# A finite-difference gradient: hand-placed semaphores and one difference pass over both rows of a tile

## The chip, the cores and the metric

The kernel runs on one core of one Trainium2 chip. The metric is the device time of a whole execution in microseconds. "Before" is the median of six runs; one execution was also recorded by the hardware profiler, and that record is the source of every duration below. The engines that matter here are VectorE (DVE), ScalarE (ACT), GpSimd (POOL) and SyncE (SP, which computes nothing and here issues loads), and the 16 DMA engines that move data between HBM and the on-chip memory SBUF.

## The reference

```python
def setup_inputs():
    return {
        "x": np.random.randn(8192, 8192).astype(np.float32),
    }

def reference(x: np.ndarray) -> np.ndarray:
    return np.gradient(x, axis=1)
```

Along each row of 8192 numbers the result is (x[j+1] - x[j-1]) / 2 inside, x[1] - x[0] at the left end and x[8191] - x[8190] at the right end. The rows don't depend on each other. 268 MB are read and 268 MB are written, with two small operations for each element.

## The kernel before

The 8192 rows are cut into 32 sets (`nsets`) of 256 rows. In a set each of the 128 partitions holds two neighbouring rows (`R = 2`), one behind the other, so a set is a tile of 128 x 16384 fp32 numbers (`W = 16384`), 64 KB in each partition and 8 MB in all. A buffer `b` of the pool has 64 more columns (`SH`): the input lies at columns 64 to 64 + W, and the result is written from column 0 on. So the result overwrites the buffer's own input, 64 columns behind the place that is being read, and one buffer serves for input and output. The pool has three such buffers (`bufs=3`); they are called slots below.

For each set, in program order:

- SP issues the load of the whole tile (line 66). The last set's load is cut into two, one for each row.
- The function `diff` works on half a row at a time (`step = m // 2`), four times for a tile, and on a quarter of a row, eight times, for the last tile. It subtracts on DVE over the inside of the piece (line 46); where the piece begins or ends a row, a one-column subtraction on DVE makes the end column (lines 39 and 52). Then ACT multiplies the inside of the piece by 0.5 in place (line 57).
- ACT issues the store of the whole tile (line 78) after its last multiplication. For the last tile it issues a store of each quarter row (line 74).

So one piece's multiplication on ACT runs while DVE subtracts the next. Loads go through SP's DMA queue and stores through ACT's. The instructions of an engine run in the order in which the program lists them (`manual_schedule`), while the waits between engines and DMAs are put in by the framework from the tiles that are read and written. A load into a slot waits until the store of the tile that the slot held three sets earlier has landed.

Of the kernel before, what the change touches and what calls it, by code (L numbers as in the profile page):

```python
# [1 line left out]

# [4 lines left out]


@with_exitstack
def kernel(  # L10
    ctx: ExitStack,
    tc: tile.TileContext,
    x: bass.AP,
    out: bass.AP,
):

    nc = tc.nc
    P = nc.NUM_PARTITIONS
    n, m = x.shape
    R = 2
    SH = 64
    W = R * m
    nsets = n // (P * R)

    x_sets = x.rearrange("(s p t) m -> s p (t m)", p=P, t=R)
    out_sets = out.rearrange("(s p t) m -> s p (t m)", p=P, t=R)  # L30

    pool = ctx.enter_context(tc.tile_pool(name="pool", bufs=3))

    def diff(b, c0, c1):

        lo, hi = c0, c1
        if c0 % m == 0:
            lo = c0 + 1
            nc.vector.tensor_sub(  # L39
                out=b[:, c0:lo],  # L40
                in0=b[:, SH + c0 + 1 : SH + c0 + 2],
                in1=b[:, SH + c0 : SH + c0 + 1],
            )
        if c1 % m == 0:
            hi = c1 - 1
        nc.vector.tensor_sub(  # L46
            out=b[:, lo:hi],
            in0=b[:, SH + lo + 1 : SH + hi + 1],
            in1=b[:, SH + lo - 1 : SH + hi - 1],
        )  # L50
        if hi < c1:
            nc.vector.tensor_sub(  # L52
                out=b[:, hi:c1],
                in0=b[:, SH + hi : SH + c1],
                in1=b[:, SH + hi - 1 : SH + c1 - 1],
            )
        nc.scalar.mul(out=b[:, lo:hi], in_=b[:, lo:hi], mul=0.5)  # L57

    with tc.manual_schedule():
        for i in range(nsets):  # L60
            last = i == nsets - 1
            b = pool.tile([P, SH + W], x.dtype)

            ls = m if last else W
            for c0 in range(0, W, ls):
                nc.sync.dma_start(  # L66
                    out=b[:, SH + c0 : SH + c0 + ls],
                    in_=x_sets[i, :, c0 : c0 + ls],
                )
            step = m // 4 if last else m // 2  # L70
            for c0 in range(0, W, step):
                diff(b, c0, c0 + step)
                if last:
                    nc.scalar.dma_start(
                        out=out_sets[i, :, c0 : c0 + step], in_=b[:, c0 : c0 + step]
                    )
            if not last:
                nc.scalar.dma_start(out=out_sets[i], in_=b[:, 0:W])


# [1 line left out]
_INS = ['x']  # L82
_OUTS = [((8192, 8192), 'float32')]


# [23 lines left out]
```

## Time and profile before

| what | value |
|---|---|
| median of six runs | 1251.67 us (1246.27 to 1253.14) |
| the profiled execution's own time | 1246.27 us |
| its span, from first to last instruction | 1244.5 us |
| bytes read and written | 268.44 MB and 268.44 MB, 431 GB/s over the span |
| DVE subtraction of 128 x 4095 (line 46) | 124 times, 4424 ns each |
| DVE one-column passes (lines 39 and 52) | 128 times, 155 and 159 ns |
| ACT multiplication of 128 x 4095 (line 57) | 124 times, 3616 ns each |
| load of 8 MB, from issue to landing | 45.2 us, median of 31 |
| store of 8 MB, from issue to landing | 48.5 us, median of 31 |
| DVE idle before line 39, waiting for a load | 640.0 us in 33 waits |
| SP waiting for a store to land before it issues a load | 1126.7 us in 29 waits |

The profiled execution is the fastest of the six. Time from issue to landing is not the time that a transfer takes alone: two transfers in two queues share the DMA engines, and one behind another in the same queue waits for it. An engine's idle time costs nothing as long as another part of the machine sets the end.

### The profile page before, as it was taken

The page shows a single profiled execution, that of the slowest core. Times are in us where ns is not written, and L with a number is a line of the kernel's source. Part 1 is how long each engine was busy: PE and PEld are TensorE (multiplying, and loading weights), DVE is VectorE, ACT ScalarE, POOL GpSimd, SP SyncE. Part 2 cuts the span into 40 slices and gives each one's busy share as a digit, 9 for nine tenths or more (in the row PEclk, how much of TensorE's full clock was granted, in tenths as well). Part 3 has the DMA queues.
Part 4 walks back from the last instruction along what each step waited for, and adds up shares of the span by engine and source line. Part 5 has one row for each costly group of instructions (what it writes and reads, how often), then busy time and mean ns, then how long its engine had stood idle before and what let it go on. Part 6 is the DMA issues. An engine that isn't in the chain of part 4 may idle for free.

```text
span 1244.5 us, 665 instructions
## 1 busy us (share of the span) xinstructions
DVE 584.5 (47%) x260; ACT 464.9 (37%) x133; POOL 0.2 (0%) x4
## 2 busy tenths in 40 slices
DVE  2950554335543355533555335553355533455353
ACT  1731442234422344323443234432344322443252
POOL 0000000000000000000000000000000000000000
DMA  9999999999999999999999999999999999999998
GB/s 404 434 438 426 421 438 434 438 438 436 426 426 436 434 438 436 438 438 436 419 432 438 434 438 436 438 436 428 428 432 434 438 436 436 438 438 423 427 433 379
DMA packets 10373, 536.92 MB, mean 431 GB/s; under 512 B 1152, under 2 KB 1152, under 8 KB 1152
## 3 DMA queue, kind: packets, MB, share of 16 engines
q1 hardware_dynamic: 4752, 268.44, 50.0%
q10 hardware_dynamic: 5616, 268.44, 49.8%
q14 instruction: 5, 0.04, 0.0%
HBM read 268.44 MB, written 268.44 MB: 431 GB/s over the span
## 4 chain that ended last, share of the span: by engine, by line
DMA 75%; DVE 16%; another core or an unknown queue 4%; ACT 3%; issue 0%; SPq 0%; DVEq 0%
DMA out_dram<-b 38%; DMA b<-in_x_dram 37%; DVE b L46 16%; ACT b L57 3%; DVE b L39 0%; DVE b L52 0%; SPq L66 0%; DVEq L39 0%
## 5 line engine op out<-in xcount | busy, mean ns | idle before, releaser
L57 ACT ACTIVATE b<-b 128x4095 f32<-128x4095 f32 (+1 forms) x132 | 463.6, 3512 | 745.3 <-DVE b L46 745.3
L46 DVE TENSOR_TENSOR b<-b 128x4095 f32<-128x4095 f32 (+1 forms) x132 | 567.0, 4295 | 4.5
L39 DVE TENSOR_TENSOR b<-b 128x1 f32<-128x1 f32 x64 | 9.9, 155 | 640.0 <-DMA b<-in_x_dram 640.0
L52 DVE TENSOR_TENSOR b<-b 128x1 f32<-128x1 f32 x64 | 10.2, 159 | 2.2
L57 ACT ACT_TABLE_LOAD x1 | 1.3, 1283 | 22.9 <-DMA b<-in_x_dram 22.9
L93 POOL MEMSET const-bfloat16-1.0<- 128x1 bf16 x1 | 0.1, 102 | 0.0
L93 POOL MEMSET const-uint8-127<- 128x1 uint8 x1 | 0.1, 102 | 0.0
L93 POOL MEMSET const-float32-0.0<- 128x1 f32 x1 | 0.1, 99 | 0.2 <-issue 0.2
L93 POOL MEMSET const-float32-1.0<- 128x1 f32 x1 | 0.1, 99 | 0.0
## 6 DMA issues: line engine op xcount, KB each, us to landing
b<-in_x_dram SPq DMA_DIRECT2D x2, 4096.0 KB, 44.9
out_dram<-b ACTq DMA_DIRECT2D x8, 1024.0 KB, 19.0
b<-in_x_dram SPq DMA_DIRECT2D x31, 45.2
out_dram<-b ACTq DMA_DIRECT2D x31, 48.5
```

Source lines behind the costliest of these rows:

```text
L39: nc.vector.tensor_sub(out=b[:, c0:lo], in0=b[:, SH + c0 + 1 : SH + c0 + 2], in1=b[:, SH + c0 : SH + c0 + 1],)
L46: nc.vector.tensor_sub(out=b[:, lo:hi], in0=b[:, SH + lo + 1 : SH + hi + 1], in1=b[:, SH + lo - 1 : SH + hi - 1],)
L52: nc.vector.tensor_sub(out=b[:, hi:c1], in0=b[:, SH + hi : SH + c1], in1=b[:, SH + hi - 1 : SH + c1 - 1],)
L57: nc.scalar.mul(out=b[:, lo:hi], in_=b[:, lo:hi], mul=0.5)
L93: nc = _bacc.Bacc("TRN2", target_bir_lowering=False, num_devices=1)
```

## The change

The three slots become three fixed tiles, and all waits are written out by hand with semaphores: `ld[k]` and `st[k]` count the landings of loads and stores of slot k, `aside`, `passed`, `halved` and `placed` count finished instructions of POOL, DVE, ACT and of the engine that places the end columns. A small tile `ends` holds the end columns of all sets, and a tile `top` takes a running maximum that nobody reads.

For each tile:

- POOL waits for the load, and computes the four end columns of a partition (two rows, left and right) in one subtraction with strided access into `ends` (`put_aside`).
- DVE waits for POOL, and makes one pass from column 1 to column 16383 of the tile, across the border between the two rows. Where two rows meet, the pass writes values that the placing replaces.
- In two tiles of three this pass is `tensor_tensor_reduce`: subtract, multiply by 0.5, write, and keep a maximum. In the third (`i % 3 == 1`) it is the plain subtraction, and ACT multiplies the whole tile in one instruction.
- POOL or ACT (`placer`) copies the four end columns from `ends` to their places.
- The store of the whole tile is issued by ACT, except for the last three sets, where SP issues it. The last set is loaded whole, worked on row by row with `tensor_tensor_reduce`, and stored row by row from SP.
- On SP, load i + 3 is issued after the program's lines for tile i, and waits for store i to land.

```diff
-    pool = ctx.enter_context(tc.tile_pool(name="pool", bufs=3))
+    pool = ctx.enter_context(tc.tile_pool(name="pool", bufs=1))
+    slots = [pool.tile([P, SH + W], f32, name=f"slot{k}", tag=f"slot{k}") for k in range(NB)]
+    ends = pool.tile([P, nsets, R, 2], f32, name="ends", tag="ends")
+    top = pool.tile([P, nsets + R], f32, name="top", tag="top")
...
+        def load(i):
+            k = i % NB
+            if st_n[k]:
+                nc.sync.wait_ge(st[k], 16 * st_n[k])
+            nc.sync.dma_start(out=slots[k][:, SH : SH + W], in_=x_sets[i]).then_inc(ld[k], 16)
+            ld_n[k] += 1
+
+        def put_aside(i):
+
+            k = i % NB
+            xin = slots[k][:, SH : SH + W].rearrange("p (t m) -> p t m", m=m)
+            nc.gpsimd.wait_ge(ld[k], 16 * ld_n[k])
+            return done(
+                nc.gpsimd.tensor_sub(
+                    out=ends[:, i, :, :],
+                    in0=xin[:, :, 1 : m : m - 2],
+                    in1=xin[:, :, 0 : m - 1 : m - 2],
+                ),
+                aside,
             )
...
+        def work(i, r0, nr, ready, by_act, placer, storer, sem):
+
+            b = slots[i % NB]
+            c0, c1 = r0 * m + 1, (r0 + nr) * m - 1
+            mid = b[:, c0:c1]
+            after = b[:, SH + c0 + 1 : SH + c1 + 1]
+            before = b[:, SH + c0 - 1 : SH + c1 - 1]
+            nc.vector.wait_ge(*ready)
+            if by_act:
+                at = done(nc.vector.tensor_sub(out=mid, in0=after, in1=before), passed)
+                nc.scalar.wait_ge(*at)
+                at = done(nc.scalar.mul(out=mid, in_=mid, mul=0.5), halved)
+            else:
+                j = i + r0
+                at = done(
+                    nc.vector.tensor_tensor_reduce(
+                        out=mid,
+                        in0=after,
+                        in1=before,
+                        scale=0.5,
+                        scalar=0.0,
+                        op0=op.subtract,
+                        op1=op.max,
+                        accum_out=top[:, j : j + 1],
+                    ),
+                    passed,
+                )
+            taken = passed[0], passed[1]
+            res = b[:, r0 * m : (r0 + nr) * m].rearrange("p (t m) -> p t m", m=m)
+            to, of = res[:, :, 0 : m : m - 1], ends[:, i, r0 : r0 + nr, :]
+            placer.wait_ge(*at)
+            copy = nc.gpsimd.tensor_copy if placer is nc.gpsimd else nc.scalar.copy
+            at = done(copy(out=to, in_=of), placed[placer])
+            storer.wait_ge(*at)
+            storer.dma_start(
+                out=out_sets[i, :, r0 * m : (r0 + nr) * m],
+                in_=b[:, r0 * m : (r0 + nr) * m],
+            ).then_inc(sem, 16)
+            return taken
 
-    with tc.manual_schedule():
+        for i in range(NB):
+            load(i)
         for i in range(nsets):
...
+            k = i % NB
+            ready = put_aside(i)
+            if i < nsets - 1:
+                by_act = i % 3 == 1
+                placer = nc.scalar if i % 3 == 2 or i % 6 == 0 else nc.gpsimd
+                storer = nc.scalar if i + NB < nsets else nc.sync
+                work(i, 0, R, ready, by_act, placer, storer, st[k])
+                st_n[k] += 1
+            else:
+                for r in range(R):
+                    ready = work(i, r, 1, ready, False, nc.gpsimd, nc.sync, st_rows[r])
+            if i + NB < nsets:
+                load(i + NB)
+        for r in range(R):
+            nc.sync.wait_ge(st_rows[r], 16)
+        for k in range(NB):
+            nc.sync.wait_ge(st[k], 16 * st_n[k])
```

## The prediction

> **What bounds the kernel now.** I read the page's head first, for who is busy, then the DMA slices and queues, then the stretch-by-stretch windows, then the chain and the timeline of single tiles.
>
> ```profile
> span 1244.5 us, 665 instructions
> DVE 584.5 (47%) x260; ACT 464.9 (37%) x133; POOL 0.2 (0%) x4
> ...
> GB/s 404 434 438 426 421 438 434 438 438 436 426 426 436 434 438 436 438 438 436 419 432 438 434 438 436 438 436 428 428 432 434 438 436 436 438 438 423 427 433 379
> ...
> q1 hardware_dynamic: 4752, 268.44, 50.0%
> q10 hardware_dynamic: 5616, 268.44, 49.8%
> q14 instruction: 5, 0.04, 0.0%
> ```
>
> The reader is to see that no engine is busy for half of the span, while the two data queues together hold the 16 DMA engines for 50.0 + 49.8 = 99.8% of it. Instruction fetches are 5 packets of 0.04 MB: shorter programs free nothing there.
>
> ```profile
> core 0: us, DVE busy (x) ACT busy (x) POOL busy (x), PEclk, DMA share, GB/s
> 22.80:42.10 19.30, 18.24 (x8) 13.12 (x5) 0.00 (x0) 1.00 1.00 435
> 1124.30:1162.90 38.60, 18.25 (x8) 14.46 (x4) 0.00 (x0) 1.00 1.00 433
> 1162.90:1201.50 38.60, 24.93 (x12) 18.28 (x6) 0.00 (x0) 1.00 1.01 434
> 1201.50:1240.20 38.70, 12.28 (x9) 11.46 (x6) 0.00 (x0) 1.00 0.98 418
> ```
>
> The first of these stretches has almost only loads, the second a load and a store side by side, and both run at 433 to 435 GB/s. So one queue with work in it fills the DMA engines as well as two do, and the last stretch, at 418, is the only one of the four that gives anything away.
>
> ```profile
> 1047.13 46.03 DMA b<-in_x_dram
> ...
> 1115.22 47.68 DMA out_dram<-b
> ```
>
> That is the chain (start, length, what), and the next is the timeline of one tile.
>
> ```profile
> 1131.88 0.16 DVE L39 TENSOR_TENSOR b<-b 128x1 f32<-128x1 f32 x1 [20.15 <-DMA b<-in_x_dram]
> ...
> 1153.82 0.34 ACTq L78 DMA_DIRECT2D out_dram<-b  x1
> ```
>
> In the chain a slot is loaded in 46.0 us, worked on for 22.0 (from 1093.2 to 1115.2) and stored in 47.7: 115.8 us, three times 38.6, because three slots take turns. The chain puts 15.7% of the span on DVE, but that is the slot's turn and not the limit. A tile's 8.39 MB passes alone in 19.3 us (the two first landings, 22.8 and 42.1), so of the 93.7 us of transfer in a turn 55 are spent sharing with the other slots. Work may lengthen by most of that before the queues run dry. The tile's data are there at 1131.9, its store is issued at 1153.8, and DVE had been idle for 20.15 us.
>
> The floor: 32 tiles x 38.6 us = 1236. The rest of the span, about 8.5 us, is some 3.5 at the head (0.7 to the first issue, and the first landing 22.1 later instead of 19.3) and some 5 at the tail and in slow slices. That is all that any change of the compute can win.
>
> [...] (4424 ns for 4095, 2292 for 2047, hence 1.041 ns an element and 0.16 us fixed). [...]
>
> **The change part by part.**
>
> *The passes.* Four DVE passes of 4424 ns and four one-column ones (157 ns) a tile become one pass of 16382 elements: 16382 x 1.041 + 0.16 = 17.2 us at full rate. Ten tiles keep ACT's multiplication, 16382 x 0.833 + 0.20 = 13.9 us (slope from 3616 and 1910 ns). In 21 tiles and the two rows of the last one the new DVE form halves as well. At full rate DVE has 32 x 17.2 = 551 us of work and ACT some 145: both fall, and neither bounds. [...] I take the full rate[...].
>
> *POOL and the placers.* A subtraction of four elements a partition, then a copy of four on POOL or ACT. The nearest rows are DVE's one-column pass (0.16) and POOL's memset (0.1); I take 0.5 us for each, with 0.2 and 3 as ends. The subtraction is new on the path from landing to store: DVE waits for POOL, and behind POOL's copy of one tile stands the subtraction of the next. On SP load i+3 still waits for store i; ACT's stores stand behind its copies and, for ten tiles, behind the 13.9 us.
>
> *The slot's turn.* Landing to store becomes 0.5 + 17.2 + 0.5 + hand-overs = about 18.7 us (22.0 before), and 18.7 + 13.9 = 33 in ACT tiles. Transfers alone need 2 x 19.3, so 115.8 - 33 - 38.6 leaves 44 us of sharing. Hidden; price nothing. Cover fails where a tile's work passes about 36 us (38.6 less the 2.8 that an empty queue needs to start, from 22.1 - 19.3): then all three slots can be without a transfer.
>
> *The head.* Tile 0 lands at 22.8, its store goes out near 41.5 (44.8 before), while load 2 is still running. Tile 1: 42.1 + 33 = 75; store 0, sharing with load 2, lasts to about 80. No gap.
>
> *The tail.* The last tile is loaded whole, and stores 29, 30 and the two rows move from ACT's queue to SP's, behind load 31. Take the old clock: at 1163.0 store 28 has landed and load 31 goes out. Load 30 is done by 1166, load 31 by 1185, stores 29 and 30 by 1224, the rows by 1234 and 1244. DVE works on tile 30 from 1166 to 1184 and on the rows to 1204, so row 0's data are ready 25 us before their turn; SP, waiting in order, holds nothing back. The stores of 1024 KB, whose 2 us windows average about 425 GB/s over 17 us, go: 0.4 us. The dip before them, 303 and 348 GB/s in 1220 to 1224, may go too: 0.5. Fewer small things in between: 0.3, by guess. Sum: -1.2 us, with 0 and -2.7 as ends (the latter is a span of 1236 + 3.5 + 2.3).
>
> *Instruction counts.* The engines' own instructions fall from 260 + 133 + 4 to 33 on DVE, 26 on ACT and 49 on POOL, with the waits beside them; the queue-14 line prices it at nothing.
>
> So the span of 1244.5 becomes 1243.3, and the profiled execution, 1246.27, 1245.1. The median of the runs, 1251.67, stands 5.4 us above that execution, which is the lowest of the six; I carry the difference over: **1250.5 us**.
>
> **The rivals.**
>
> *Half-rate pass (slower).* Passes of 34.3 us. Start: tile 0's store goes out at 22.8 + 0.5 + 34.3 + 0.5 = 58, load 2 ends at 61, store 0 at about 80; tile 1, behind tile 0 on DVE and then on ACT, is ready only at 89, so DMA is empty until load 3 starts: 2.8 us, and once more a turn later. Tail: tile 30's pass ends at 1201, row 0 at 1218, row 1 at 1235.5, after its turn at 1234; with placing and a restart about 4 us lost. Sum 2 x 2.8 + 4 - 1.2 = +8: **1259.5**. It decides from 25 us a pass at the start (54.9 + the pass against 80) and 33 at the tail.[...]
>
> *POOL late.* A subtraction or copy that takes 6 us or more[...] brings ACT tiles to 39 us, past the 36. Two or three restarts, 3 to 8 us: **1256**.[...]
>
> *More won than the span shows (faster).* The whole tail goes, -2.7, and of the 5.4 us that ordinary runs have over the profiled one some belong to the many small instructions: **1246.5**. Nothing in the trace shows such a share.
>
> **How the numbers follow.** Hidden, no change: 0.54. Half rate: 0.22. POOL late: 0.10. Faster: 0.14. About 0.3%, or 3.8 us, is what a measurement here tells from nothing; the first case lies within it (own range 1248 to 1253), the second and third are slower, the fourth faster: 0.14, 0.54, 0.32. The range of 1246 to 1260 holds the first and third, most of the fourth and half of the second.
>
> **What would show it.** Right: slices of 430 to 438 GB/s to the end, no dip in the first 130 us, a reducing pass near 17.2 us, DVE idle before landings, last stores back to back. Wrong: a pass near 34 us, POOL lines of several us in the chain, DMA slices below 400 near 80, 120 or 1234 us.

## The result

The changed kernel is slower: 1264.01 us median against 1251.99, ratio 1.0083 with an interval of 1.0067 to 1.0098. The forecast was 1250.5 us, no change that can be measured, and its range ended at 1260: it missed on both counts. The profiled execution of the changed kernel took 1263.34 us with a span of 1261.5, 17.0 us more than the span of before. Medians here and below are over all runs, while the ratios leave out runs more than 1.5% above the fastest of their kernel (6 of the changed kernel's 31, none of the 67 before), so the two need not agree to the last tenth of a per cent.

The first view is the head of the page and its DMA slices, of the changed kernel.

```profile
span 1261.5 us, 256 instructions
DVE 551.5 (44%) x56; ACT 143.0 (11%) x27; POOL 18.4 (1%) x53
...
GB/s 401 430 432 432 432 432 432 432 424 436 434 432 432 432 432 432 430 405 441 438 438 384 434 432 418 401 432 432 409 432 436 434 414 434 434 432 432 399 401 397
...
q1 hardware_dynamic: 5184, 293.60, 54.5%
q10 hardware_dynamic: 4176, 243.27, 45.0%
```

DVE and ACT do less than before, POOL's work is 1% of the span, and the program has 256 instructions instead of 665. The same bytes are moved, but at 426 GB/s over the span instead of 431: slices of 405, 384, 401, 409 and 414 stand among slices of 432, some three or four slices (of 31.5 us) apart, and the last three are near 400. So time is lost in the transfers, in places, and not to a compute engine that works too long.

It is not lost mainly by DMA engines that stand idle. The two queues' packets hold them for 54.5 + 45.0 = 99.5% of 1261.5 us, that is 1255 us; before it was 99.8% of 1244.5, or 1242 us. So about 13 of the 17 us are packets that take longer for the same bytes. The windows of the long middle part (us, busy of DVE, ACT and POOL, clock, DMA share, GB/s), before and after, say the same: the share is 1.00 in both, and less is moved.

```profile
150.00:1150.00 1000.00, 474.05 (x207) 372.43 (x103) 0.00 (x0) 1.00 1.00 434
150.00:1150.00 1000.00, 440.16 (x42) 127.06 (x21) 7.69 (x39) 1.00 1.00 428
```

The next view is the groups by line with shapes kept apart (busy us, mean ns of one, idle before).

```profile
L102 DVE CUSTOM_DVE_ANT_0 slot<-slot 128x16382 f32<-128x16382 f32 x21 | 361.7, 17224 | 461.1 <-POOL ends L79 461.1
L96 DVE TENSOR_TENSOR slot<-slot 128x16382 f32<-128x16382 f32 x10 | 172.2, 17224 | 201.4 <-POOL ends L79 201.4
L98 ACT ACTIVATE slot<-slot 128x16382 f32<-128x16382 f32 x10 | 138.5, 13854 | 576.8 <-DVE slot L96 576.8
...
L119 POOL COPY slot<-ends 128x2 f32<-128x2 f32 x2 | 8.9, 4447 | 8.8 <-DVE top L102 8.8
L79 POOL TENSOR_TENSOR ends<-slot 128x4 f32<-128x4 f32 x32 | 6.4, 200 | 793.7 <-DMA slot<-in_x_dram 793.7
...
L119 POOL COPY slot<-ends 128x4 f32<-128x4 f32 x15 | 2.9, 192 | 398.7 <-ACT slot L98 312.1 <-DVE top L102 86.7
```

The new one-pass form takes 17224 ns, to the nanosecond as long as the plain subtraction of the same size: the half-rate rival is out. POOL's small operations take 0.2 us: the rival of a late POOL is out for the whole tiles too. On whole tiles every operation of the sum had the forecast duration within 0.3 us, and the sum was still wrong.

Two of the places, in windows of one tile's DMA time, with the same columns:

```profile
738.00:776.60 38.60, 17.22 (x1) 6.27 (x1) 0.20 (x1) 1.00 1.00 431
776.60:815.20 38.60, 17.23 (x2) 7.78 (x2) 0.39 (x2) 1.00 0.95 389
815.20:853.90 38.70, 17.23 (x2) 0.00 (x0) 0.39 (x2) 1.00 1.00 434
853.90:892.50 38.60, 17.23 (x1) 4.05 (x1) 0.20 (x1) 1.00 1.00 433
892.50:931.10 38.60, 17.23 (x2) 10.00 (x2) 0.39 (x2) 1.00 0.98 406
```

In this stretch two of the five windows move less, and they are those in which ACT finishes a whole tile. At 389 GB/s about 10% is missing, while the DMA share is only 5% lower. The chain runs through that tile's slot, slot 1, in every turn:

```profile
708.99 43.78 DMA slot<-in_x_dram
...
753.07 17.23 DVE slot L96
...
770.33 13.86 ACT slot L98
...
784.47 42.17 DMA out_dram<-slot
826.65 44.24 DMA slot<-in_x_dram
...
902.59 42.53 DMA out_dram<-slot
```

This turn, from store to store, is 902.59 - 784.47 = 118.1 us; before, the median is 115.9. The work in it grew from 22.0 to 31.7 us, and load and store together shrank only from 93.7 to 86.4. Turns differ: the nine between the ten stores of slot 1 take 12.1 us more than before in all, and a single one up to 3.9.

How late that store is shows in the timeline, of ACT's and SP's DMA issues. SP's line is the load that waits for the previous tile's store, so it tells when that one landed. First the changed kernel, then the kernel before:

```profile
784.47 0.34 ACTq L121 DMA_DIRECT2D out_dram<-slot  x1
...
786.52 0.33 SPq L70 DMA_DIRECT2D slot<-in_x_dram  x1
```

```profile
766.65 0.34 ACTq L78 DMA_DIRECT2D out_dram<-b  x1
...
776.60 0.33 SPq L66 DMA_DIRECT2D b<-in_x_dram  x1
```

Before, the next store was put in the queue 10.0 us ahead of the landing of the one in front of it; now it is 2.1 us. I call this the lead of a store. Its median over eight turns of slot 1 is 10.0 us before and 1.9 after; the two tiles without ACT have 16.8. While the stores' queue has no next transfer, only one load moves, and it is about to end too (at 791.5 us in this turn): its successor waits for the same store.

Two microseconds are too few, as the single packets in the traces show (each belongs to the DMA engine whose previous packet ended when it began). A packet of 64 KB usually holds one DMA engine for 2418 ns. Half of the 16 engines have moved their last packet of a store 4.5 us (before) or 6.5 us (slot 1 now, both medians) ahead of the landing that SP waits for. So when slot 1's store is issued now, 15 or 16 engines have no store packet left, half of them for 2.1 to 8.1 us already; before, it was never more than two engines. The packets after such a restart take up to 4.3 us. Between the head and the tail (tiles 3 to 28), in the 18 us after each issue of slot 1, what packets take beyond 2418 ns adds up to 0.4 to 2.0 us for each DMA engine; for the other two tiles, and for all tiles before, to 0.2 at most. So an empty stores' queue goes with slow packets more than with idle engines.

### The profile page after: what moved, and what is told of

It reads as the page before. It is cut to its first block, busy times and chain, and to the rows that moved or that the text cites. A ratio compares the mean times of both kernels' runs of the same rounds, so it can differ in the third digit from the quotient of the medians.

```text
span 1261.5 us, 256 instructions
## 1 busy us (share of the span) xinstructions
DVE 551.5 (44%) x56; ACT 143.0 (11%) x27; POOL 18.4 (1%) x53
## 3 DMA queue, kind: packets, MB, share of 16 engines
q1 hardware_dynamic: 5184, 293.60, 54.5%
## 4 chain that ended last, share of the span: by engine, by line
DMA 70%; DVE 14%; ACT 11%; POOL 1%; issue 0%; SPq 0%
DMA slot<-in_x_dram 36%; DMA out_dram<-slot 34%; DVE slot L96 14%; ACT slot L98 11%; POOL slot L119 1%; DVE slot L102 1%; POOL ends L79 0%; SPq L70 0%; SPq L172 0%; DVE top L102 0%; SPq L46 0%
## 5 line engine op out<-in xcount | busy, mean ns | idle before, releaser
L102 DVE CUSTOM_DVE_ANT_0 slot<-slot 128x16382 f32<-128x16382 f32 (+1 forms) x23 | 379.1, 16482 | 466.7 <-POOL ends L79 466.6
L96 DVE TENSOR_TENSOR slot<-slot 128x16382 f32<-128x16382 f32 x10 | 172.2, 17224 | 201.4 <-POOL ends L79 201.4
L98 ACT ACTIVATE slot<-slot 128x16382 f32<-128x16382 f32 x10 | 138.5, 13854 | 576.8 <-DVE slot L96 576.8
L119 ACT COPY slot<-ends 128x4 f32<-128x4 f32 x16 | 3.2, 198 | 476.1 <-DVE top L102 476.1
L79 POOL TENSOR_TENSOR ends<-slot 128x4 f32<-128x4 f32 x32 | 6.4, 200 | 793.7 <-DMA slot<-in_x_dram 793.7
L119 POOL COPY slot<-ends 128x4 f32<-128x4 f32 (+1 forms) x17 | 11.8, 692 | 407.6 <-ACT slot L98 312.1
```

What stands on the lines that cost most here:

```text
L79: nc.gpsimd.tensor_sub(out=ends[:, i, :, :], in0=xin[:, :, 1 : m : m - 2], in1=xin[:, :, 0 : m - 1 : m - 2],),
L96: at = done(nc.vector.tensor_sub(out=mid, in0=after, in1=before), passed)
L98: at = done(nc.scalar.mul(out=mid, in_=mid, mul=0.5), halved)
L102: nc.vector.tensor_tensor_reduce(out=mid, in0=after, in1=before, scale=0.5, scalar=0.0, op0=op.subtract, op1=op.max, accum_out=top[:, j : ...
L119: at = done(copy(out=to, in_=of), placed[placer])
```

## The experiments

The theory after the result (A): with one whole pass and one whole multiplication behind each other, slot 1's store comes too late to keep the stores' queue filled, and each turn loses for it; a smaller part is lost where the last stores stand behind a load on SP. The rivals: the hand-placed order and POOL's place ahead of DVE (B), the one-pass form disturbing the transfers (C), ACT's traffic in the slot (D). All ratios are against the kernel before.

### Without ACT's multiplication

```diff
-                by_act = i % 3 == 1
+                by_act = False
```

> All 31 whole tiles take the one-pass form, none ACT's multiplication, so landing to store is about 18.7 us in every tile instead of 31.7 in one of three. Theory A (the 31.7 us tile comes out of its turn too late, the stores' queue runs dry once a turn): the loss of a turn goes, some 13 of the 17 us of the span, only the tail's 3 stay: ratio 1.000 to 1.003, span about 1248, turn of slot 1 115.8 us. Theory B (hand-placed order, POOL ahead of each DVE pass, and loads that are issued after the program's lines of a tile): all of these are unchanged, so ratio 1.007 to 1.009. Theory C (the one-pass form on DVE disturbs the transfers): more of it, so 1.010 or above.

Measured: 1252.63 us median, ratio 1.0007 (0.9982 to 1.0031), span 1250.3. Lead of slot 1: 16.0 us, turns of 116 us. The middle part moves as much as before:

```profile
150.00:1150.00 1000.00, 446.79 (x51) 2.37 (x12) 7.62 (x39) 1.00 1.00 434
```

The loss of the turns is gone, with the order of all other instructions and POOL's part unchanged and ten more one-pass forms: B and C fall.

### ACT's tile in four pieces

```diff
-                at = done(nc.vector.tensor_sub(out=mid, in0=after, in1=before), passed)
-                nc.scalar.wait_ge(*at)
-                at = done(nc.scalar.mul(out=mid, in_=mid, mul=0.5), halved)
+                n4 = -(-(c1 - c0) // 4)
+                for q in range(0, c1 - c0, n4):
+                    if q:
+                        nc.vector.wait_ge(passed[0], passed[1])
+                    e = min(q + n4, c1 - c0)
...
+                    nc.scalar.wait_ge(*at)
+                    at = done(nc.scalar.mul(out=mid[:, q:e], in_=mid[:, q:e], mul=0.5), halved)
```

> ACT's tile is subtracted and multiplied in four pieces, so that the two engines overlap; ACT's work stays 13.9 us, landing to store falls from 31.7 to about 22 us. Theory A: as without ACT, ratio 1.000 to 1.003. Theory B: 1.007 to 1.009. Theory D (ACT's multiplication itself, by its reads and writes of the slot, slows the DMAs): 1.007 or more, since all of it is still there.

Measured: 1251.9 us, ratio 0.999 (0.9972 to 1.0007). The timeline of such a tile, whose data landed at 746.1:

```profile
746.37 17.81 DVE L102 TENSOR_TENSOR slot<-slot 128x4096 f32<-128x4096 f32 x4 [21.66 <-POOL ends L79]
750.83 3.62 ACT L108 ACTIVATE slot<-slot 128x4096 f32<-128x4096 f32 x1 [25.89 <-DVE slot L102]
...
768.11 0.34 ACTq L131 DMA_DIRECT2D out_dram<-slot  x1
```

ACT does all of its work, beside DVE instead of behind it; 22.0 us from landing to store, lead 11.7. D falls: what costs is that the two stand one behind the other.

### The same length with ACT at work elsewhere

```diff
-                by_act = i % 3 == 1
+                by_act = False
...
             taken = passed[0], passed[1]
+            if nr == R and i % 3 == 1:
+                nc.scalar.wait_ge(*at)
+                for _ in range(13):
+                    at = done(nc.scalar.mul(out=idle[:, :], in_=idle[:, :], mul=0.5), halved)
+                    nc.scalar.wait_ge(*at)
```

`idle` is a tile of 128 x 1024 that nothing else uses.

> All tiles take the one-pass form; in one of three ACT then multiplies a small tile aside 13 times (about 1.05 us each with the waits between), before the end columns are placed, so that landing to store is again about 32 us without ACT touching the slot. Theory A: as slow as the changed kernel, ratio 1.006 to 1.010, a dip in the DMA slices once a turn. Theory C or D: not slower than without ACT, 1.000 to 1.003 (D).

Measured: 1264.6 us, ratio 1.0103 (1.0073 to 1.0133), just above the forecast range, with 32.0 us from landing to store. Time alone, spent outside the slot, brings the whole loss back.

### The long tile in the kernel before

```diff
-            step = m // 4 if last else m // 2
+            step = m // 4 if last else W if i % 3 == 1 else m // 2
```

> The kernel before, with one tile in three subtracted in one pass and multiplied in one instruction; the two end columns where the rows of such a tile meet are left out. Landing to store is about 31.5 us there and 22 elsewhere; nothing else of the change is in it. Theory A: slower than before by what the turns lose, ratio 1.005 to 1.009. Theory B: no change, 0.999 to 1.001.

Measured: 1263.57 us, ratio 1.0083 (1.0049 to 1.0117), the same as the changed kernel. Nothing of the change is in it but the whole passes of every third tile (groups by line, shapes apart):

```profile
L46 DVE TENSOR_TENSOR b<-b 128x16382 f32<-128x16382 f32 x10 | 172.2, 17224 | 0.3
L57 ACT ACTIVATE b<-b 128x16382 f32<-128x16382 f32 x10 | 138.5, 13854 | 325.0 <-DVE b L46 325.0
```

Lead of slot 1: 2.4 us. The loss needs neither the semaphores nor POOL nor the one-pass form.

### A shorter and a longer delay

The kernel with the multiplications aside again, with 9 and with 18 of them.

> As with 13 multiplications aside, but 9 of them: landing to store about 28 us in one tile of three. Theory A with about 29 us to spare: no turn is lost, ratio 1.000 to 1.003, as without padding. If the loss grows evenly with the work from 19 us on: about two thirds of what 13 cost, 1.006 to 1.007.

> 18 multiplications aside: landing to store about 38 us in one tile of three. Theory A with about 29 us to spare: each of ten turns loses about 8 us, 80 us in all, ratio 1.05 to 1.08. If the loss grows evenly with the work from 19 us on: 1.014.

Measured: 9 give 1252.93 us, ratio 1.0008 (0.999 to 1.0027); 18 give 1275.73 us, ratio 1.0165 (1.0119 to 1.0212). In the timelines the data of a tile lie there at 747.4 and 757.8, and then (9 first, 18 second):

```profile
764.93 9.76 ACT L121 ACTIVATE idle<-idle 128x1024 f32<-128x1024 f32 x9 [38.86 <-DVE top L105]
774.75 0.19 POOL L127 COPY slot<-ends 128x4 f32<-128x4 f32 x1 [27.12 <-ACT idle L121]
775.03 0.34 ACTq L129 DMA_DIRECT2D out_dram<-slot  x1
```

```profile
775.33 19.55 ACT L121 ACTIVATE idle<-idle 128x1024 f32<-128x1024 f32 x18 [45.84 <-DVE top L105]
794.94 0.19 POOL L127 COPY slot<-ends 128x4 f32<-128x4 f32 x1 [36.91 <-ACT idle L121]
795.22 0.34 ACTq L129 DMA_DIRECT2D out_dram<-slot  x1
```

27.6 us from landing to store (median lead 5.4 us) cost nothing, 31.6 cost what the changed kernel lost, so the edge lies between the two. The size beyond it was missed: at 37.4 us, where the store is issued after the previous one has landed (median lead -4.8 us), a turn loses (1.0165 - 1.0007) x 1252 / 10 = 2.0 us and not 8. Lateness is not paid one to one; in the changed kernel's turn above, load and store got shorter while the work grew. The changed kernel, by the same sum, loses 0.95 us a turn.

### The last stores left with ACT

```diff
-                storer = nc.scalar if i + NB < nsets else nc.sync
+                storer = nc.scalar
...
-                    ready = work(i, r, 1, ready, False, nc.gpsimd, nc.sync, st_rows[r])
+                    ready = work(i, r, 1, ready, False, nc.scalar, nc.scalar, st_rows[r])
```

Once beside the kernel without ACT's multiplication, once in the changed kernel itself.

> As the first of these kernels (one-pass form in all tiles), and the last three sets' stores stay in ACT's queue instead of going to SP's; ACT also places the end columns of the last two rows. Theory A with a tail part: store 29 no longer stands behind load 31, which waits for store 28, so the DMA engines don't run dry there; some 4 to 6 us of the 1250.3 us span go, span about 1245, ratio 0.995 to 0.998 against before. If the tail's order costs nothing: span about 1250, ratio 1.000 as without this edit.

> The changed kernel, ACT's multiplication of one tile in three kept, with the last three sets' stores and the last end columns left with ACT. The dip behind store 28 goes, the loss of the turns stays: about 4 us less than the changed kernel, span about 1257, ratio 1.004 to 1.006. If the tail's order were the main loss after all: 1.000 or below.

Measured: the first, 1249.86 us, ratio 0.9989 (0.9968 to 1.0011), span 1246.0; the second, 1264.0 us, ratio 1.0064 (1.0036 to 1.0092). Without ACT's multiplication, the windows of the tail with the stores on SP, and then on ACT:

```profile
1162.90:1201.50 38.60, 27.70 (x5) 0.20 (x1) 2.14 (x3) 1.00 0.87 357
```

```profile
1162.90:1201.50 38.60, 17.23 (x2) 0.20 (x1) 0.20 (x1) 1.00 1.00 433
```

The dip of the tail is SP's order, and it is worth 4.3 us of span between these two profiles. In the timed runs both ratios move the right way (1.0007 to 0.9989, 1.0083 to 1.0064), less far than forecast, and the intervals overlap; the changed kernel's median does not move at all. So the price in the ratio is not settled.

### Every tile by ACT

```diff
-                by_act = i % 3 == 1
+                by_act = True
```

> Every whole tile is subtracted by DVE in one plain pass and multiplied by ACT in one instruction, so that landing to store is about 31.7 us in all of them; the last set stays in the one-pass form. If each tile that takes longer than about 29 us leaves the stores' queue dry by some 1.3 us, 31 of them instead of 10 cost about 40 us: ratio 1.025 to 1.035. If only the contrast between one long tile and two short ones matters (uneven turns), an even 31.7 us costs nothing: 1.000 to 1.003.

Measured: 1258.17 us, ratio 1.0065 (1.0045 to 1.0085). A miss for both. Median leads are 2.1 to 2.7 us in all slots, and yet 31 long tiles cost no more than 10 among short ones. A loss for each long tile is the wrong rule; how uneven the tiles are has a part in it. The packets show which: here half of the DMA engines have been without a store packet for only 1.4 to 2.9 us when a store is issued, and slow packets add 0.0 to 0.8 us after it. By and large it costs more the longer the stores' queue has been empty: in slot 1 of the changed kernel 0.4 us after 2.3 us, and 2.0 after 8.1.

### A row stored early

```diff
+                taken = passed[0], passed[1]
+                for r in range(R):
+                    lo, hi = r * m + 1, (r + 1) * m - 1
+                    nc.scalar.wait_ge(*taken)
+                    at = done(nc.scalar.mul(out=b[:, lo:hi], in_=b[:, lo:hi], mul=0.5), halved)
...
+                    storer.wait_ge(*at)
+                    storer.dma_start(
+                        out=out_sets[i, :, r * m : (r + 1) * m],
+                        in_=b[:, r * m : (r + 1) * m],
+                    ).then_inc(sem, 16)
```

> The changed kernel, but in ACT's tiles the first row is multiplied, completed and stored before ACT multiplies the second, in two DMAs of 4 MB. DVE's pass stays whole, the slot is still worked on for about 32 us, the tail stays with SP; the first bytes of the store leave after about 24.5 us. If what costs is the stores' queue with nothing in it (theory A): the loss of the turns goes, ratio 1.000 to 1.003, turns of 116 us. If it is the length of the slot's whole work, or the unevenness of the tiles' work in itself: 1.007 to 1.010.

Measured: 1252.3 us, ratio 1.0013 (0.9991 to 1.0035). In the timeline of ACT's tile (data at 746.9) and of SP:

```profile
771.72 0.34 ACTq L112 DMA_DIRECT2D out_dram<-slot  x1
...
779.41 0.34 ACTq L112 DMA_DIRECT2D out_dram<-slot  x1
```

```profile
778.60 0.33 SPq L70 DMA_DIRECT2D slot<-in_x_dram  x1
```

The slot is worked on for 32.6 us, longer than in the changed kernel, beside two short tiles as before; only its first half reaches the queue 6.9 us ahead of the previous landing, and the loss is gone. So neither the length of the work nor the unevenness costs by itself: what costs is a stores' queue that has run empty.

### Smaller pieces

```diff
-            nc.sync.dma_start(out=slots[k][:, SH : SH + W], in_=x_sets[i]).then_inc(ld[k], 16)
+            for r in range(R):
+                nc.sync.dma_start(
+                    out=slots[k][:, SH + r * m : SH + (r + 1) * m],
+                    in_=x_sets[i, :, r * m : (r + 1) * m],
+                ).then_inc(ld[k], 16)
```

and the same for the stores.

> The changed kernel with each load and store issued as two DMAs, one a row, so that a DMA engine moves 32 KB at a time instead of 64 KB before it turns to the other queue. Theory A in its finer form (the time left for a tile is shorter than 38.6 us because a landing and a start each wait for whole 64 KB turns of the other queue, 2.4 us each): the time left grows by about 3 us, past 31.7, so the turn of slot 1 goes from 118 back to about 116 us; the smaller pieces themselves cost some 4 us over the span (1213 ns for 32 KB against 2418 for 64), so ratio 1.003 to 1.006. If the size of a turn has no part in it: the loss of the turns stays and the 4 us are added, ratio 1.010 to 1.013.

Measured: 1279.89 us, ratio 1.0208 (1.0164 to 1.0253), worse than either case, in four runs. That a DMA engine mostly turns to the other queue after one packet is in the traces: before, between 150 and 1150 us, 5034 of 6605 packets follow one of the other queue, and a packet takes 2418 ns for 64 KB and 1213 for the 32 KB of a row's load. The smaller pieces did not lengthen the time left: in one turn the data lay there at 640.4 us, the load that waits for the previous store's landing went out at 671.8, and the tile's own store only at 672.0. Why halves cost this much was not followed up.

## Why the prediction was wrong, step by step

- **The bound.** Right: the DMA engines, busy for 99.5% of the span as they were for 99.8%. Not foreseen was that they can move less while busy: 428 GB/s instead of 434 in the middle part.
- **The passes and the placers.** Right in size and in rank: 17.22 us where 17.2 was forecast, 13.85 where 13.9 was, and 0.2 for POOL where 0.5 was taken. The half rate of the slower rival, a pass of 34.3 us from twice the 1.041 ns an element of the plain subtraction, was an assumption of mine that no trace had shown: the one-pass form and the plain subtraction take 17224 ns each. "No engine bounds" held as well.
- **The slot's turn: the step that failed.** It said "Hidden; price nothing", and put the edge at "about 36 us", from the mean period of 38.6. The delays put it between 27.6 and 31.6 us. The prediction's own lines held a better number: a tile's data were there at 1131.9, and the store ahead of it, issued at 1115.2, landed 47.7 us later, at 1162.9. So 31.0 us were left until that landing, and the forecast of 33 us for an ACT tile was already past them. The changed kernel's turn above leaves 33.7 us (752.8 to 786.5), but half of the DMA engines run out of store packets some 6.5 us before a landing. By this estimate about 27 us are of use, and the work takes 31.6. I had counted 44 us of sharing as if any of it could be given up. But a load that runs beside stores lands late (before, 45.2 us after its issue, the median, where the first load, with no store beside it, took 22.1), and what is left after it is fixed by when the store in front ends. The term priced at nothing is 0.95 us for each of ten turns; in the profiles, 1261.5 - 1250.3 = 11.2 us.
- **The head.** Tile 0's store went out at 40.5 us, forecast 41.5, and nothing was lost there.
- **The tail.** "SP, waiting in order, holds nothing back" was wrong. The end columns of tile 29 were placed at 1158.0, but its store stood in SP's queue behind load 31, which waited for store 28 (timeline of the changed kernel; the second line covers all four of SP's stores, the first of which it starts with):

```profile
1157.83 0.20 ACT L119 COPY slot<-ends 128x4 f32<-128x4 f32 x1 [21.22 <-DVE top L102]
...
1179.26 41.35 SPq L121 DMA_DIRECT2D out_dram<-slot  x4
```

  For 21 us tile 29 was ready, and nothing stood behind store 28 in a queue of stores. It ran out: the stretch from 1162.9 to 1178.9 moved 393 GB/s and the one from there to 1183.0 only 304. I had followed what each store waits for, and not which landing the waiting load in front of it waits for. Where the sum had -1.2 us, the profiles without ACT's multiplication put about +4 on the tail's order.
- **Instruction counts.** The price of nothing was right. The count for DVE was not: 56 instead of 33, because each of the 23 one-pass forms is followed by a read of its maximum, of 83 ns.
- **The rivals.** Each of the slower ones looked for an operation that takes too long. The slower side came true without one, by operations of the forecast length that stand one behind the other. The rival of a late POOL came nearest, since it saw that ACT's tiles could pass an edge, but it needed 6 us of POOL for that. The faster case found nothing to stand on.

By one profiled execution of each kernel, 11.2 of the 17.0 us of span are the turns, 4.3 the tail's order, and 1.5 remain (1246.0 against 1244.5), which is within what executions of one kernel differ by. The split is rough: the tail's window that moved 357 GB/s without ACT's multiplication moves 406 in the changed kernel, which suggests that the tail costs less there and the turns more. A version with both mended, at 0.9989 (0.9968 to 1.0011), is not told apart from the kernel before: the fewer and larger instructions win nothing that these runs can show.

What stays open: why the packets are slow after the stores' queue has run empty on most DMA engines. That the two go together is shown turn by turn; the mechanism is not.

## What to carry to other kernels

Where transfers are the bound, don't compare a tile's work with the mean period: read from the trace how long after a tile's landing the previous store lands, and keep several microseconds of that in hand for the next store (here 5.4 us were enough and 2.4 were not). A DMA share of 1.00 doesn't prove that nothing is lost: look at the GB/s beside it (here 428 against 434, at 1.00 in both). Pieces that let two engines overlap, or an early store of the first half, kept the queue filled here at no cost that shows (ratios 0.999 and 1.0013); the fewer and larger instructions of the change emptied it (1.0083). When issues move to another queue, follow for each one which landing the instruction in front of it waits for.

## What the runs showed besides

GpSimd's copy of the end columns took 0.2 us everywhere but in the last tile, where DVE started a pass with two inputs just before it:

```profile
1210.90 8.69 DVE L102 CUSTOM_DVE_ANT_0 slot<-slot 128x8190 f32<-128x8190 f32 x1
1210.93 8.92 POOL L119 COPY slot<-ends 128x2 f32<-128x2 f32 x2 [8.80 <-DVE top L102]
```

The first of the two copies lasted until that pass was over, 8.7 us. In the kernel without ACT's multiplication it is the same (8.69 us for the pass, 8.92 for the two copies). What ties the copy to the pass is not shown. Where ACT placed these columns beside the same pass (with the last stores left to ACT), its copy took 0.20 us. Whether the longer copy cost time here was not tried.
